# Turning over the expert product of a fused transformer block: activations held, rows of peer_v moving

## The chip, the cores and the metric

The program runs on one core of one Trainium2 chip. The metric is the device time of one launch in microseconds (us). The engines are TensorE (PE, matmuls; PEld is its weight load), VectorE (DVE), ScalarE (ACT), GpSimd (POOL) and the queue of SyncE (SP), which issues most of the loads.

## The reference, cut to what matters

Two transformer blocks in sequence on 512 tokens of width 1024. The part that the change touches is the first block's expert layer (PEER): 16384 experts, each a row of `peer_u` and a row of `peer_v`, both 16384 x 1024, seen as 128 keys of 128 experts. For each token, eight heads pick 16 experts each, with a softmax gate g over the 16. With h the normalised input, the layer adds to the residual

```
x += sum over the chosen experts e of  g[e] * gelu(h . peer_u[e]) * peer_v[e]
```

For one block of 128 tokens the kernel gathers only the chosen rows. For the other 384 tokens it computes the products of all 16384 experts densely, with a gate of zero for those not chosen: first u = gelu(peer_u h), then w = gate x u, then the sum over experts of w times peer_v.

## The kernel before, in words

Everything is kept transposed: x is eight tiles of 128 channels x 512 tokens. Products are float32 made of pairs of fp32r: a value is split into a rounded high part and the rest, and `mm3` (L236) does three matmuls, high x high, high x low and low x high, into one PSUM bank. `wchunk` (L206) loads 128 x 1024 weights (`wraw`, three buffers), copies the high part on ScalarE (`whi`, L214) and takes the difference on VectorE (`wlo`, L215). PSUM has eight banks, handed out by tag: mm 2, S 2, L 2, T 1, st 1 (L89).

`phase_b` (L714) does the expert layer in two stages.

The spill stage: routing on VectorE picks experts and builds the gates of all keys, which are written to DRAM (`Gd`, in 12 writes of 2 MB); meanwhile `u_spill` computes the u products of 68 keys (the first 68, 24 matmuls of 384 columns each) and writes them to DRAM (`Sd`).

The experts stage: `v_group` (L990) handles four keys. It reads their gates (`gt`, 0.75 MB in runs of 512 bytes), reads back the spilled activations (`gr`) or takes those just computed (`gs`), multiplies by the gates (L1002, alternately on VectorE and GpSimd), and splits the result into `whi_` and `wlo_` (L1005, L1006). Then for each of the eight channel chunks m it holds a 128 x 128 piece of peer_v (`pv`, laid out for this on the host) and moves the 384 token columns of the four keys' activations past it: 4 keys x 3 matmuls into one bank S or L, and then one addition to x on VectorE (L1017). 32 groups make 256 such additions. The u products of the other 60 keys (`u_tile`) are woven in between by step counts, and groups of spilled and of fresh keys alternate.

Beside both stages runs `gather` (L914) for the first 128 tokens: an indirect DMA on GpSimd's queue fetches 128 rows (`row`, L927, four buffers), and VectorE multiplies and sums (L938, L945). `weave` advances it by the ratio VR of the costs that the main loop yields, and `pace` ties each of its instructions to a matmul already recorded.

The last group's additions feed the next norm chunk by chunk (`nf.add`: high part and square on ScalarE, difference and sum on VectorE), and the feed-forward stage follows. Instructions are recorded in the order of the generators; at build time a planner orders each engine's instructions by recorded order and by when its own model has their inputs ready. Engines then work in that order.

Of the kernel before, what the change touches and what calls it, by code (L numbers as in the profile page):

```python
# [7 lines left out]
F32 = mybir.dt.float32  # L8
F32R = mybir.dt.float32r
# [4 lines left out]
AF = mybir.ActivationFunctionType  # L14
OP = mybir.AluOpType
# [7 lines left out]
T = 512  # L23
# [15 lines left out]

CAND = [(a, b) for a in range(16) for b in range(16) if (a + 1) * (b + 1) <= 16]  # L40
NC = len(CAND)
GS = 4
NG = 128 // GS
# [12 lines left out]
PT = 12  # L56
SO = 0.5
TB = 8
BC = 2600
GSC = 32768.0  # L60
# [113 lines left out]
class Kern:  # L174
# [539 lines left out]
    def phase_b(self, n2):  # L714
        nc, I, x = self.nc, self.I, self.x
        ACT, V, G = nc.scalar, nc.vector, nc.gpsimd
        ND = T - TG
        NTB = ND // 32
        dp = self.ctx.enter_context(self.tc.tile_pool(name="dram", bufs=1, space=DRAM))
        Gd = dp.tile([NTB, 128, 128, 32], F32, name="gates")  # L720
        Sd = dp.tile([SPILL, 128, ND], F32, name="spill")
        eg = ExitStack()
        gp_ = eg.enter_context(self.pool("gath", "right"))
        er = ExitStack()
# [2 lines left out]
        rp = erq.enter_context(self.pool("route", "right"))  # L727
# [43 lines left out]
        rp = er.enter_context(self.pool("route2", "right"))  # L771
# [4 lines left out]
        spilled = {}  # L776
# [137 lines left out]
        def gather():  # L914

            g2 = gsel0.rearrange("p h s -> p (h s)")
            acc = gp_.tile([128, 1024], F32, name="gacc")
            V.memset(acc, 0.0)
            dots = gp_.tile([128, 128], F32, name="dots")
            junk = gp_.tile([128, 1024], F32, name="junk")  # L920
# [12 lines left out]
            for n, (tab, s) in enumerate(seq):  # L933
                if n + ROWB - 1 < len(seq):
                    issue(n + ROWB - 1)
                row = rows.pop(n)
                if tab == "u":
                    self.pace(V.scalar_tensor_tensor(junk, row, 1.0, hnat, op0=OP.mult, op1=OP.mult,  # L938
                                                     accum_out=dots[:, s:s + 1]), BACK)
                    if s % 16 == 15:  # L940
                        ss = slice(s - 15, s + 1)
                        ACT.activation(dots[:, ss], dots[:, ss], AF.Gelu_apprx_tanh)
                        V.tensor_tensor(dots[:, ss], dots[:, ss], g2[:, ss], op=OP.mult)
                else:
                    self.pace(V.scalar_tensor_tensor(acc, row, dots[:, s:s + 1], acc, op0=OP.mult, op1=OP.add), BACK)  # L945
                yield 1170
            for k in range(2):
                pt = self.ps("T")
                for q in range(4):
                    m = 4 * k + q  # L950
                    nc.tensor.transpose(pt[:, q * 128:(q + 1) * 128], acc[:, m * 128:(m + 1) * 128], self.ident)
                for q in range(4):
                    m = 4 * k + q
                    V.tensor_tensor(x[m][:, :TG], x[m][:, :TG], pt[:, q * 128:(q + 1) * 128], op=OP.add)
                yield 800

        def u_tile(j, pool, spill):
            ps = self.ps("mm")
            yield from self.proj_g(ps, I["u"][j], hhi, hlo, n=ND, cost=490)
            g = pool.tile([128, ND], F32, name="gs", bufs=3 if spill else 2 * GS)  # L960
            ACT.activation(g, ps[:, :ND], AF.Gelu_apprx_tanh)
            if spill:
                ACT.dma_start(Sd[j], g)
            spilled[j] = None if spill else g
            yield 0

        def u_spill():
            for j in range(SPILL):
                yield from u_tile(j, rp, True)

        gat = gather()

# [14 lines left out]
        ev = ExitStack()  # L987
        vp = ev.enter_context(self.pool("vph", "right"))

        def v_group(g, last):  # L990
            gt = vp.tile([128, NTB, GS, 32], F32, name="gt", bufs=2)
            nc.sync.dma_start(gt.rearrange("p a j t -> p a (j t)"),
                              Gd[:, :, g * GS:(g + 1) * GS, :].rearrange("a p j t -> p a (j t)"))
            W = []
            for q in range(GS):
                j = g * GS + q
                s = spilled[j]
                if s is None:
                    s = vp.tile([128, ND], F32, name="gr", bufs=4)
                    nc.sync.dma_start(s, Sd[j])  # L1000
                s3 = s.rearrange("p (a t) -> p a t", t=32)
                (G if q % 2 else V).tensor_tensor(s3, s3, gt[:, :, q, :], op=OP.mult)  # L1002
                a = vp.tile([128, ND], F32R, name="whi_", bufs=2 * GS)
                c = vp.tile([128, ND], F32R, name="wlo_", bufs=2 * GS)
                ACT.activation(a, s, AF.Copy)  # L1005
                V.tensor_tensor(c, s, a.bitcast(F32), op=OP.subtract)  # L1006
                W.append((a, c))
            for mp in range(4):
                whi, wlo = self.wchunk(I["pv"][g, mp].rearrange("p m j d -> p (m j d)"), 1024)
                for m2 in range(2):  # L1010
                    m = 2 * mp + m2
                    ps = self.ps("L" if m2 else "S")
                    for q in range(GS):
                        o = slice((m2 * GS + q) * 128, (m2 * GS + q + 1) * 128)
                        self.mm3(ps[:, :ND], (whi[:, o], wlo[:, o]), W[q], q == 0, q == GS - 1)
                        yield 490
                    V.tensor_tensor(x[m][:, TG:], x[m][:, TG:], ps[:, :ND], op=OP.add)  # L1017
                    if last:
                        nf.add(m, x[m])

        nf = Norm(self, "f1")
        sg = list(range(SPILL // GS))
        ug = list(range(SPILL // GS, NG))
        seq = []
        ns, nu = len(sg), len(ug)
        a = b = 0
        while a < ns or b < nu:
            if a < ns and (b >= nu or (a + SO) * nu <= b * ns):
                seq.append(sg[a])
                a += 1  # L1030
            else:
                seq.append(ug[b])
                b += 1

        def u_all():
            for g in ug:
                for q in range(GS):
                    yield from u_tile(g * GS + q, vp, False)

        def main():  # L1040
            ugen = u_all()
            total = nu * GS * 9
            vsteps = NG * GS * 8
            done, vdone = 0, 0
            for n, g in enumerate(seq):
                need = (ug.index(g) + 1) * GS * 9 if g in ug else 0
                while done < need:
                    yield next(ugen, 0)
                    done += 1
                if n == len(seq) - 1:  # L1050
                    yield None
                for c in v_group(g, n == len(seq) - 1):
                    yield c
                    vdone += 1
                    while done < total and done * vsteps < vdone * total * 1.08:
                        yield next(ugen, 0)
                        done += 1
            for c in ugen:
                yield c

        weave(main(), gat, VR)
        ev.close()
# [487 lines left out]
def layout(i):  # L1550

    f = lambda n: np.asarray(i[n])
# [33 lines left out]
    r["pv"] = c(f("peer_v")[0].reshape(NG, GS, 128, 4, 2, 128).transpose(0, 3, 2, 4, 1, 5))  # L1586
# [73 lines left out]
```

## Time and profile before

| | us |
|---|---|
| median of 3 runs | 2904.09 (2901.44 to 2911.04) |
| the profiled execution | 2895.47 |
| its span, first to last instruction | 2893.7 |
| PE busy | 2810.8 |
| DVE busy | 2011.0 |
| ACT busy | 1158.4 |
| POOL busy | 477.3 |

The profile is one execution. Busy time is the time in which an engine had an instruction; for PE the instructions overlap, and their ends are modelled, so a busy PE can still lose time between starts. Idle time is put down to the event that came last before the waiting instruction. The granted clock of PE (PEclk) is 1.0 at 2.4 GHz and 0.5 at 1.2 GHz, averaged over a stretch. The DMA share is the mean busy share of 16 DMA engines, and can come out a little above 1.

### The profile page before, as it was taken

What the parts mean: (1) busy time and instruction counts of PE and PEld (TensorE: products, weight loads), DVE (VectorE), ACT (ScalarE), POOL (GpSimd) and SP (SyncE); (2) the same over time, 40 slices, a digit from 0 to 9 for tenths busy, and PEclk for the clock granted to TensorE, in tenths of its full rate; (3) what the DMA queues carried; (4) which work ended last, traced back from release to release, by engine and by line L of the source; (5) the groups of instructions that cost most, each with busy time, mean ns of one, the idle gap of its engine ahead of it and who ended that gap; (6) DMA issues with size and microseconds to landing.
All of it is one profiled execution on the core that took longest, in us unless ns stands there. A gap on an engine that the chain in (4) does not pass through costs nothing. (4 is left out here: it accounts for less than half of the span.)

```text
span 2893.7 us, 38745 instructions
## 1 busy us (share of the span) xinstructions
PE 2810.8 (97%) x14599; PEld 2432.8 (84%) x14599; DVE 2011.0 (69%) x3932; ACT 1158.4 (40%) x1719; POOL 477.3 (16%) x350
## 2 busy tenths in 40 slices
PE   8999999999899998999999999999999999999999
PEld 6678777788799998999999999998888866688887
DVE  6752466679999997889898898974443467544432
ACT  5742344333365663333333333342322355533221
POOL 0000000000042234444444444400000000000000
PEclk9999999999899999999999999999999998999999
DMA  4223211332387889999888898833223311122232
GB/s 167 66 75 113 68 52 52 107 104 81 111 313 249 304 310 350 319 305 318 312 304 311 306 311 294 288 120 101 96 93 93 99 66 44 59 95 95 96 103 79
DMA packets 188956, 494.02 MB, mean 171 GB/s; under 512 B 15968, under 2 KB 84704, under 8 KB 187104
## 3 DMA queue, kind: packets, MB, share of 16 engines
q1 hardware_dynamic: 140384, 318.76, 33.2%
q0 software_dynamic: 36864, 134.23, 13.3%
q10 hardware_dynamic: 11520, 38.54, 3.4%
q8 instruction: 115, 1.88, 0.3%
q14 instruction: 73, 0.60, 0.1%
HBM read 450.84 MB, written 40.63 MB: 170 GB/s over the span
## 5 line engine op out<-in xcount | busy, mean ns | idle before, releaser
L214 ACT ACTIVATE whi<-wraw 128x1024 fp32r<-128x1024 f32 x524 | 546.5, 1044 | 1259.4 <-PE mm L239 623.4
L240 PE MATMUL mm<-hhi,wlo 128*128 128x512 f32 (+1 forms) x2272 | 843.9, 372 | 34.9 <-DVE wlo L215 34.8
L238 PE MATMUL mm<-hhi,whi 128*128 128x512 f32 (+1 forms) x2272 | 854.7, 376 | 19.4 <-ACT whi L214 9.0
L239 PE MATMUL mm<-hlo,whi 128*128 128x512 f32 (+1 forms) x2272 | 841.5, 370 | 0.0
L215 DVE TENSOR_TENSOR wlo<-wraw,whi 128x1024 fp32r<-128x1024 f32 x524 | 640.5, 1224 | 241.7 <-ACT whi L214 238.6
L240 PEld LDWEIGHTS mm<-hhi,wlo 128*128 128x128 f32 x2272 | 432.1, 190 | 93.3 <-DVE wlo L215 42.1
L238 PEld LDWEIGHTS mm<-hhi,whi 128*128 128x128 f32 x2272 | 432.5, 190 | 76.6 <-ACT whi L214 10.1
L239 PEld LDWEIGHTS mm<-hlo,whi 128*128 128x128 f32 x2272 | 432.3, 190 | 49.4 <-issue 3.6
L927 POOL DMA_INDIRECT row<-u_nat,eidx x128 | 193.7, 1513 | 584.4 <-PE mm L239 327.9
L927 POOL DMA_INDIRECT row<-v_nat,eidx x128 | 188.3, 1471 | 247.7 <-PE mm L240 56.6
L945 DVE SCALAR_TENSOR_TENSOR gacc<-row,dots,gacc 128x1024 f32<-128x1024 f32 x128 | 171.7, 1342 | 20.8 <-DMA row<-v_nat,eidx 11.1
L938 DVE SCALAR_TENSOR_TENSOR junk<-row,hnat 128x1024 f32<-128x1024 f32 x128 | 164.3, 1284 | 12.6 <-DMA row<-u_nat,eidx 6.6
L238 PE MATMUL mm<-fhi,whi 128*128 128x512 f32 x352 | 139.1, 395 | 0.0
L240 PE MATMUL mm<-fhi,wlo 128*128 128x512 f32 x352 | 139.0, 395 | 0.0
L239 PE MATMUL mm<-flo,whi 128*128 128x512 f32 x352 | 139.0, 395 | 0.0
L884 ACT ACTIVATE stg<-L 128x512 f32<-128x512 f32 x96 | 100.4, 1155 | 46.7 <-PE L L881 37.5
L1083 DVE TENSOR_TENSOR fu<-mm,nbc 128x512 f32<-128x512 f32 x40 | 27.7, 691 | 127.0 <-PE mm L240 127.0
L1079 DVE TENSOR_TENSOR fg<-mm,nbc 128x512 f32<-128x512 f32 x40 | 27.7, 691 | 85.6 <-PE mm L240 84.2
L1017 DVE TENSOR_TENSOR x<-x,L 128x384 f32<-128x384 f32 x128 | 70.2, 548 | 18.5 <-PE L L240 18.1
L240 PEld LDWEIGHTS mm<-fhi,wlo 128*128 128x128 f32 x352 | 66.0, 187 | 16.2
L239 PEld LDWEIGHTS mm<-flo,whi 128*128 128x128 f32 x352 | 66.0, 187 | 16.2
L238 PEld LDWEIGHTS mm<-fhi,whi 128*128 128x128 f32 x352 | 66.0, 187 | 16.1
(2376 smaller groups left out, 4772.5 us busy)
## 6 DMA issues: line engine op xcount, KB each, us to landing
wraw<-u SPq DMA_DIRECT2D x128, 512.0 KB
wraw<-pv SPq DMA_DIRECT2D x128, 512.0 KB
gates<-stg ACTq DMA_DIRECT2D x12, 2048.0 KB
gt<-gates SPq DMA_DIRECT2D x32, 768.0 KB
spill<-gs ACTq DMA_DIRECT2D x68, 192.0 KB
gr<-spill SPq DMA_DIRECT2D x68, 192.0 KB
wraw<-w_f1g SPq DMA_DIRECT2D x22, 512.0 KB
wraw<-w_f1u SPq DMA_DIRECT2D x22, 512.0 KB
```

The source lines that it names most:

```text
L214: nc.scalar.activation(hi[:, :n], raw[:, :n], AF.Copy)
L215: (nc.gpsimd if pool_lo else nc.vector).tensor_tensor(lo[:, :n], raw[:, :n], hi[:, :n].bitcast(F32), op=OP.subtract)
L238: nc.tensor.matmul(ps, a[0], b[0], start=start, stop=False)
L239: nc.tensor.matmul(ps, a[0], b[1], start=False, stop=False)
L240: self.mms.append(nc.tensor.matmul(ps, a[1], b[0], start=False, stop=stop).ins.name)
L884: ACT.activation(stg[:, :, o:o + 4].rearrange("p j t -> p t j"), gp.rearrange("p (t j) -> p t j", t=4), AF.Copy, scale=1.0 / GSC)
L927: self.pace(G.indirect_dma_start(out=rows[n], out_offset=None, in_=I[tab + "_nat"], in_offset=bass.IndirectOffsetOnAxis(ap=eidx[:, s:s + 1 ...
L938: self.pace(V.scalar_tensor_tensor(junk, row, 1.0, hnat, op0=OP.mult, op1=OP.mult, accum_out=dots[:, s:s + 1]), BACK)
L945: self.pace(V.scalar_tensor_tensor(acc, row, dots[:, s:s + 1], acc, op0=OP.mult, op1=OP.add), BACK)
L1017: V.tensor_tensor(x[m][:, TG:], x[m][:, TG:], ps[:, :ND], op=OP.add)
L1079: V.tensor_tensor(g, pg, n.bc, op=OP.mult)
L1083: V.tensor_tensor(u, pu, n.bc, op=OP.mult)
```

## The change

The experts stage is turned over. For each key, a 128 x 128 piece of its activations (128 experts x 128 tokens, three pieces for 384 tokens) is held, and the 512 columns of half a row block of peer_v move past it. The result is tokens x channels, in six banks (three token blocks x two halves; tags S, L, T and S, L, st), summed over all 128 keys in PSUM. At the end the six banks are copied out (alternately ScalarE and VectorE), transposed back in 24 pieces of 128 x 128 on TensorE, and added to x in eight additions. The last three keys do the first half of the channels for all three, then the second.

With it: gates are read for eight keys at a time (1.5 MB, runs of 1024 bytes); all gate products are on VectorE; activations are prepared one key at a time, three keys ahead of their product, and loaded four keys before that; the spilled keys are the first four of each eight and the last four, 68 as before; u products are spread over the keys with a lead of 48 steps. The gather has five row buffers in place of four, writes its product over the row instead of into a tile of its own, and takes bank mm for its transposes; VR goes from 0.345 to 0.335. The copy of peer_v laid out on the host is no longer needed.

```diff
-GS = 4
-SPILL = 68
+GS = 8
+PREP = 3
+LEAD = 48
+TAIL = 3
-ROWB = 4
+ROWB = 5
-VR = 0.345
+VR = 0.335
 ...
+        def slot(j):
+            return j % GS < GS // 2 or j >= T_ALL - GS // 2
 ...
+        def gates_in(g):
+            gts[g] = vp.tile([128, NTB, GS, 32], F32, name="gt", bufs=GTB)
+            nc.sync.dma_start(gts[g].rearrange("p a j t -> p a (j t)"),
                               Gd[:, :, g * GS:(g + 1) * GS, :].rearrange("a p j t -> p a (j t)"))
+        def act_in(j):
+            if slot(j):
+                acts[j] = vp.tile([128, ND], F32, name="gr", bufs=7)
+                nc.sync.dma_start(acts[j], Sd[j])
+        def prep(j):
+            s = acts.pop(j)
+            s3 = s.rearrange("p (a t) -> p a t", t=32)
+            V.tensor_tensor(s3, s3, gts[j // GS][:, :, j % GS, :], op=OP.mult)
+            a = vp.tile([128, ND], F32R, name="whi_", bufs=WB)
+            c = vp.tile([128, ND], F32R, name="wlo_", bufs=WB)
+            ACT.activation(a, s, AF.Copy)
+            V.tensor_tensor(c, s, a.bitcast(F32), op=OP.subtract)
+            W[j] = a, c
+        Y = [[self.ps(t) for t in tags] for tags in (("S", "L", "T"), ("S", "L", "st"))]
+        def v_part(j, h, b):
+            a, c = W[j]
+            whi, wlo = chunks[j]
+            o, bs = slice(h * 512, h * 512 + 512), slice(b * 128, b * 128 + 128)
+            st, sp = j == 0, j == T_ALL - 1
+            y = Y[h][b]
+            nc.tensor.matmul(y, a[:, bs], whi[:, o], start=st, stop=False)
+            nc.tensor.matmul(y, a[:, bs], wlo[:, o], start=False, stop=False)
+            self.mms.append(nc.tensor.matmul(y, c[:, bs], whi[:, o], start=False, stop=sp).ins.name)
 ...
+        def y_add(m):
+            h, q = divmod(m, 4)
+            ps = self.ps("mm")
+            for b in range(3):
+                nc.tensor.transpose(ps[:, b * 128:(b + 1) * 128], yn[h, b][:, q * 128:(q + 1) * 128], self.ident)
+            V.tensor_tensor(x[m][:, TG:], x[m][:, TG:], ps[:, :ND], op=OP.add)
+            nf.add(m, x[m])
 ...
+            n_v = T_ALL - TAIL
+            gates_in(0)
+            loaded = prepped = 0
+            for n in range(n_v + 1):
+                if n < n_v:
+                    if n % GS == GS // 2 and n // GS + 1 < NG:
+                        gates_in(n // GS + 1)
+                    last = T_ALL if n == n_v - 1 else min(n + PREP + 1, T_ALL)
+                    while loaded < min(T_ALL, last + 4):
+                        act_in(loaded)
+                        loaded += 1
+                    while prepped < last:
 ...
+                        prep(j)
+                        prepped += 1
+                if n < n_v:
+                    chunk(n)
+                    for i in range(6):
+                        v_part(n, i // 3, i % 3)
+                        yield 680
+                        yield from u_to(int(len(here) * 8 * min(1.0, (n * 6 + i + LEAD) / (T_ALL * 6))))
+                    del chunks[n]
```

## Rows read from the trace of the kernel before

**Rows 1.** The page: span, and busy time and share of each engine.
```profile
span 2893.7 us, 38745 instructions
...
PE 2810.8 (97%) x14599; PEld 2432.8 (84%) x14599; DVE 2011.0 (69%) x3932; ACT 1158.4 (40%) x1719; POOL 477.3 (16%) x350
```

**Rows 2.** Busy time by stretch: stretch, length, busy (instructions), PEclk, DMA share, GB/s.
```profile
1097.00:1135.00 38.00, 27.99 (x132) 26.83 (x131) 24.71 (x26) 10.64 (x17) 15.63 (x13) 0.82 1.03 377
1135.00:1745.00 610.00, 597.11 (x3396) 590.21 (x3396) 550.22 (x731) 213.37 (x291) 287.85 (x214) 1.00 0.90 310
1745.00:1773.00 28.00, 22.96 (x118) 22.13 (x118) 20.83 (x26) 6.42 (x8) 10.54 (x9) 0.88 0.82 283
1773.00:1912.00 139.00, 138.69 (x800) 138.21 (x799) 118.80 (x164) 49.75 (x67) 48.38 (x35) 1.00 0.74 257
...
1097.00:1927.00 830.00, 801.75 (x4526) 792.33 (x4525) 728.11 (x965) 291.17 (x399) 362.40 (x269) 0.99 0.87 300
```

**Rows 3.** Timeline of PE: start, length, engine, line; each pair starts ten matmuls apart.
```profile
1503.15 0.33 PE L239 MATMUL mm<-hlo,whi 128*128 128x384 f32 x1
...
1504.88 0.33 PE L240 MATMUL mm<-hhi,wlo 128*128 128x384 f32 x1
...
261.67 0.39 PE L240 MATMUL L<-whi,hlo 128*128 128x512 f32 x1
...
263.94 0.39 PE L238 MATMUL S<-whi,hhi 128*128 128x512 f32 x1
...
565.18 0.39 PE L238 MATMUL mm<-ahi,whi 128*128 128x512 f32 x1
...
567.51 0.39 PE L239 MATMUL mm<-alo,whi 128*128 128x512 f32 x1
```

**Rows 4.** Waits of PE, 1135 to 1912 us: total us, times, longest.
```profile
PE mm L240 <- DVE wlo L215: 4.4, 2, 3.1
PE S L240 <- DVE wlo L215: 3.2, 4, 1.9
PE S L238 <- ACT whi__11157 L1005: 1.3, 1, 1.3
...
PE S L238 <- ACT whi__13831 L1005: 0.2, 1, 0.2
```

**Rows 5.** Groups of instructions, 1097 to 1927 us: count, busy, mean ns, idle before.
```profile
L1017 DVE TENSOR_TENSOR x<-x,S 128x384 f32<-128x384 f32 x128 | 70.0, 547 | 7.7 <-PE S L240 7.3
...
L1002 POOL TENSOR_TENSOR gr<-gr,gt 128x384 f32<-128x384 f32 x34 | 43.2, 1272 | 80.7 <-DMA gr<-spill 64.2 <-issue 9.8 <-DVE wlo L215 4.0
...
L1002 DVE TENSOR_TENSOR gs<-gs,gt 128x384 f32<-128x384 f32 x30 | 16.5, 551 | 0.0
```

**Rows 6.** Timeline at the end of the stage and in the next norm.
```profile
1926.57 0.39 PE L238 MATMUL mm<-hhi,whi 128*128 128x512 f32 x1
...
1929.00 0.55 DVE L1017 TENSOR_TENSOR x<-x,L 128x384 f32<-128x384 f32 x1
...
1931.26 0.69 DVE L150 TENSOR_TENSOR acc<-acc,sq 128x512 f32<-128x512 f32 x1
...
1939.53 0.65 PE L169 MATMUL T<-consts,nrn 128*128 128x128 f32 x4
```

**Rows 7.** Timeline at the start of the stage.
```profile
1104.57 0.39 SPq L992 DMA_DIRECT2D gt<-gates  x1
...
1109.02 0.69 PE L240 MATMUL mm<-hhi,wlo 128*128 128x384 f32 x1 [6.90 <-DVE wlo L215]
...
1111.74 0.43 SPq L992 DMA_DIRECT2D gt<-gates  x1
...
1114.78 0.55 DVE L1002 TENSOR_TENSOR gs<-gs,gt 128x384 f32<-128x384 f32 x1
...
1123.45 0.34 PE L238 MATMUL S<-whi__10644,whi 128*128 128x384 f32 x1
```

**Rows 8.** Timeline of VectorE in the disturbed stretch.
```profile
1751.34 0.56 DVE L1002 TENSOR_TENSOR gr<-gr,gt 128x384 f32<-128x384 f32 x1 [2.74 <-DMA gt<-gates]
```

More of the change, by code (lines that the diff above doesn't have):

```diff
@@ L720, in phase_b @@
         Gd = dp.tile([NTB, 128, 128, 32], F32, name="gates")
-        Sd = dp.tile([SPILL, 128, ND], F32, name="spill")
+        Sd = dp.tile([T_ALL, 128, ND], F32, name="spill")
         eg = ExitStack()
@@ L947, in gather @@
             for k in range(2):
[L948 removed]
+                pt = self.ps("mm")
                 for q in range(4):
@@ L959, in u_tile @@
             yield from self.proj_g(ps, I["u"][j], hhi, hlo, n=ND, cost=490)
-            g = pool.tile([128, ND], F32, name="gs", bufs=3 if spill else 2 * GS)
+            g = pool.tile([128, ND], F32, name="gs", bufs=3 if spill else 8)
             ACT.activation(g, ps[:, :ND], AF.Gelu_apprx_tanh)
@@ L965, in u_tile @@
             yield 0
+        def slot(j):
+            return j % GS < GS // 2 or j >= T_ALL - GS // 2
         def u_spill():
-            for j in range(SPILL):
-                yield from u_tile(j, rp, True)
+            for j in range(T_ALL):
+                if slot(j):
+                    yield from u_tile(j, rp, True)
         gat = gather()
@@ L1021, in phase_b @@
-        nf = Norm(self, "f1")
[L1022 to L1030, printed above, removed]
-            else:
[L1032 to L1038, printed above, removed]
+        order = list(range(T_ALL))
@@ new lines, in phase_b @@
+        here = [j for j in order if not slot(j)]
+        gts, acts, W, chunks = {}, {}, {}, {}
+        def gates_in(g):
+            gts[g] = vp.tile([128, NTB, GS, 32], F32, name="gt", bufs=GTB)
+            nc.sync.dma_start(gts[g].rearrange("p a j t -> p a (j t)"),
+                              Gd[:, :, g * GS:(g + 1) * GS, :].rearrange("a p j t -> p a (j t)"))
+        def act_in(j):
+            if slot(j):
+                acts[j] = vp.tile([128, ND], F32, name="gr", bufs=7)
+                nc.sync.dma_start(acts[j], Sd[j])
@@ new lines, in prep, with chunk @@
+        def prep(j):
[7 more added lines that the diff above has]
+            W[j] = a, c
+        def chunk(j):
+            chunks[j] = self.wchunk(I["v_nat"][j * 128:(j + 1) * 128], 1024)
@@ new lines, in phase_b, with y_out @@
+        yn = {}
+        def y_out(h, b):
+            if not yn:
+                yn["t"] = vp.tile([128, NTB, GS, 32], F32, name="gt", bufs=GTB)
+            t = yn["t"].rearrange("p a j t -> p (a j t)")[:, (3 * h + b) * 512:(3 * h + b + 1) * 512]
+            if (h + b) % 2:
+                V.tensor_copy(t, Y[h][b])
+            else:
+                ACT.activation(t, Y[h][b], AF.Copy)
+            yn[h, b] = t
+        def y_add(m):
[5 more added lines that the diff above has]
+            nf.add(m, x[m])
@@ L1040, in main, with u_all @@
         def main():
+            def u_all():
+                for j in here:
+                    yield from u_tile(j, vp, False)
+                    acts[j] = spilled[j]
             ugen = u_all()
[L1042 to L1052, printed above, removed]
-                    yield c
[L1054 to L1057, printed above, removed]
@@ L1058, in main, with u_to @@
-            for c in ugen:
-                yield c
+            done = [0]
+            def u_to(n):
+                while done[0] < n:
+                    c = next(ugen, None)
+                    if c is None:
+                        return
+                    done[0] += 1 if c else 0
+                    yield c
+            n_v = T_ALL - TAIL
[10 more added lines that the diff above has]
+                    while prepped < last:
+                        j = prepped
+                        if not slot(j):
+                            yield from u_to((here.index(j) + 1) * 8)
+                            for c in ugen_end(ugen, j):
+                                yield c
+                        prep(j)
[7 more added lines that the diff above has]
+                    del chunks[n]
@@ new lines, in main @@
+            tail = list(range(n_v, T_ALL))
+            yield None
+            for h in range(2):
+                for j in tail:
+                    if h == 0:
+                        chunk(j)
+                    for b in range(3):
+                        v_part(j, h, b)
+                        yield 680
+                    if h == 1 and j < tail[-1]:
+                        m = j - n_v
+                        y_add(m)
+                for b in range(3):
+                    y_out(h, b)
@@ L1061, in phase_b, with ugen_end @@
+            for m in range(TAIL - 1, 4):
+                y_add(m)
+            for m in range(4, 8):
+                y_add(m)
+        def ugen_end(g, j):
+            while j not in acts:
+                c = next(g, None)
+                yield c or 0
         weave(main(), gat, VR)
```

38 lines of the change are left out of this document (4 added, 34 removed).

## The prediction

> **What bounds the kernel now.** The page comes first: TensorE is busy for 97% of a span of 2893.7 us, VectorE for 69% [rows 1], and the DMA engines, in the longest part of the changed stage, for 0.90 [rows 2]. So whatever this change gives must be TensorE time: either fewer cycles of streaming, or shorter waits of TensorE. A table by stretches then splits the experts stage, 1097 to 1927 us, into its start, two long quiet parts with a disturbed stretch between them, and the end; in each the reader is to compare the number of matmuls with the time [rows 2]. For that I need the time of one matmul in an undisturbed stream, which the durations don't give (they overlap); the starts of successive matmuls do: ten matmuls of 384 columns take 1504.88 - 1503.15 = 1.73 us, so one takes 173.4 ns (the starts are rounded; I use 173.4) [rows 3]. Then 4526 matmuls need 784.8 us of the 830, and 45 us are lost. By stretch (time less number times 173.4 ns): 15 at the start, 21 in the first long part, 7.5 in 1745 to 1773, 0.3 after it [rows 2]. TensorE's own waits between 1135 and 1912 name what is late: eleven waits of 0.2 to 1.3 us (10.6 in sum; the first and the last row are shown) for the copy of a key's activations (whi_ of L1005), and six (7.6 us) for a weight split on VectorE [rows 4].
>
> **The change, part by part.**
>
> *Streaming.* Before, 32 groups x 8 chunks x 4 keys x 3 = 3072 matmuls of 384 columns; after, 128 keys x 2 halves x 3 token blocks x 3 = 2304 of 512. The columns are the same, 1,179,648, so only what a matmul costs beyond its columns can be saved. The trace has the new shape already: in the attention's v projection a weight chunk of 512 columns moves past 128 token columns of activations, and ten matmuls take 263.94 - 261.67 = 2.27 us, 227 ns each; another stream of 512 columns (the branch projection) takes 2.33 us for ten, 233 ns [rows 3]. At the full level of 2.4 GHz, at which this stretch runs, 384 and 512 columns are 160 and 213.3 ns, so about 13.4 ns are left over in both shapes. 3072 x 173.4 = 532.7 us becomes 2304 x 226.7 = 522.3: a gain of 10.4 us. With the slower of the two streams it is 2304 x 233 = 536.8, a loss of 4.1. I take the first, since there a weight chunk is what moves, as here.
> [...]
>
> *Residual adds.* The 256 additions of 384 columns from PSUM (two groups of 128, one of them shown, 0.547 us each) go: 140 us of VectorE [rows 5]. In their place stand six copies out of PSUM, 24 transposes and eight additions at the end. Four transposes in a row took 0.65 us from the first start to the last end [rows 6], so 24 are at most 3.9 us more on TensorE; I take 3, as the last end hangs over.
>
> *Gate products.* The 64 products on GpSimd (1.27 us each in the group shown) go to VectorE at 0.55 us, +35 us there [rows 5]. VectorE, 728 us busy in this stage [rows 2], falls to about 728 - 140 + 35 = 623, from 88% to some 77%. By itself this is worth nothing, since VectorE doesn't set the end. It pays through the queue: the weight splits stand behind less.
>
> *Waits of the long parts.* Activations are now prepared three keys ahead, one key at a time, while four at once were needed at each group's start; three keys are 3 x (18 x 0.227 + 11 x 0.173) = 18 us of TensorE work, and the chain behind one key (a product, a copy and a difference of 384 columns, the product 0.55 us long [rows 5]) is short against that. So I take the 10.6 us of group starts as gone. Of the 7.6 us of waits for splits I keep 3. The rest of the 28.8 us lost there (28.8 - 18.2 = 10.6: half-clock time after the 1754 us wait and matmuls a few ns late) I keep to 7. That leaves 10 in place of 28.8. Bounds: 3 (only the kept waits), and above, all of 28.8 and the bursts of the third rival.
>
> *Gates by eight keys.* 16 reads of 1.5 MB instead of 32 of 0.75. Runs of 1024 bytes in place of 512 may move faster; I count nothing, as the DMA share in the quiet part is 0.90 [rows 2] and it is the waiting, not the sum, that could hurt. SP's queue holds behind each read the loads of spilled activations (seven buffers, so seven keys deep) and the weight chunks (three raw buffers). A product that waits for its gates also holds up the splits behind it on VectorE, and TensorE waits for those.
>
> *Start of the stage.* Before, four u tiles were recorded first and the gates were wanted only afterwards. The gates' read went out at 1104.57, after the last gates write; TensorE stood 6.9 us for a split at 1109.02 (at half clock after it); the first v product came at 1123.45 [rows 7]. After, the first key's preparation stands first, and needs 1.5 MB through a DMA that is full (share 1.03, 377 GB/s [rows 2]). The first 0.75 MB were used at 1114.78, 10 us after the issue [rows 7]; twice as much lands some 2 to 4 us later, and the first product could go at about 1119. The order on an engine is not the recorded one: the second group's read went out at 1111.74, ahead of the first group's products, which are recorded before it [rows 7]. So the u tiles that are recorded next (30 steps of 3 matmuls, 15.6 us) can be put ahead of the first product and fill 1097 to 1113. So about the same 15 us are lost. Bounds: 8 (no wait for the split) and 26 (TensorE does one or two u tiles and then stands until 1119, with half clock after it).
>
> *End.* Before, the residual adds of the last group ran beside its matmuls; the last one came at 1929.00, the last norm sum at 1931.26, and the FFN's first matmuls had begun at 1926.57: TensorE never stood [rows 6]. After, four of eight chunks can only be added when the last matmul is through; each needs an addition (0.55), a split's difference and a norm sum (0.69 [rows 6], and I take as much for the difference), so 1.9 us of VectorE, 8 us in all, with the last copies out of PSUM ahead of them. What hides it is the FFN over the first four chunks: 4 x 3 x 0.227 = 2.7 us for each weight chunk, three chunks at hand. If the planner uses all three it is covered, if none it costs 8 to 9 us: I take 3.
>
> The spill stage before 1097 us writes 68 tiles as before, only others; the in-place product and the fifth row buffer cost nothing there, since the instructions stay the same in number and size, and a row that comes earlier can only shorten a wait.
>
> **Sum.** Streaming 784.8 - 532.7 + 522.3 + 3 = 777.4; waits 15 + 10 + 3 = 28; 805 us in place of 830: 25 us less. The profiled execution took 2895.5 us (span 2893.7 and 1.8 around it), so after it 2870. The median of the runs shown is 2904.1, 8.6 above the profiled one; I predict a median, so 2904 - 25 = 2879 us.
>
> **Rivals.**
> 1. *The streaming saves nothing.* The moving chunk meets the slower cadence of 233 ns (536.8 instead of 522.3, +14.5); what the waits give remains. For it: one of the two streams of 512 columns runs so; against it: the one in which weights move doesn't [rows 3]. 805 + 14.5 = 819.5, 10.5 gained: 2894 us, on the edge of what can be told. Chance 0.16; half of that falls within 0.3%.
> 2. *The waits of the long parts were the DMA's.* With share 0.90 the loads are late whatever VectorE does, and 28.8 us stay in place of 10: 19 less gain, 2898 us, no change. For it: in 1745 to 1773 VectorE itself waited 2.74 us for gates [rows 8]. Against it: TensorE's waits name the preparation of keys much more often [rows 4]. Chance 0.10.
> 3. *Slower: each gates read stops the pipe.* A read of 1.5 MB alone takes about 4 us at 377 GB/s, 8 or more beside row and chunk loads; if the product waits for it, the splits behind it wait, TensorE stands for over 3 us and then runs at half clock. That is what happened once, at 1745 to 1773: a product 2.74 us late for its gates [rows 8], TensorE 3.1 us late for a split [rows 4], granted clock 0.88, 7.5 us lost [rows 2]. A read is recorded only one key (6 us) before its first use. On all 15 later reads it would be 112 us (2991), on six 45 (2924); from four on (30 us) the gain is gone. Against it: SP issues a read as soon as the buffer two groups back is free, some eight keys earlier, as the read at 1111.74 shows [rows 7]. Chance 0.13.
>
> **How the numbers follow.** Forecast 0.61, rivals 0.16, 0.10, 0.13. 2879 is the forecast's time. Its own bounds: all in favour (start 8, middle 3, end 0) is 17 less, 2862; start 26 and end 9 give 17 more, 2896. To hold 8 in 10 the range takes in the first two rivals and the beginning of the third: 2857 to 2908. A measurement of this kernel can tell about 0.3% (8.7 us) from no change: below 2895 is faster, above 2913 slower. Faster: most of the forecast and half of the first rival, 0.68; within: 0.17; slower: 0.15.
>
> **What would show it.** Right: ten v matmuls of 512 columns in 2.27 us; no waits of TensorE for whi_ of the key activations; GpSimd without products; VectorE near 77% in the stage; TensorE's waits in the middle under 10 us; the stage near 805 us. Wrong: 2.33 us for ten; waits of VectorE for gates of several us, followed by half-clock stretches, at every eighth key; a gap of over 15 us ahead of the first v product, or of over 6 after the last.

## The result, and the profile of the changed kernel

The change made the kernel slower: a median of 2940.8 us over four runs (2938.2 to 2953.5) against 2903.9 us for the kernel before beside it, a ratio of 1.0141 (95% interval 1.0118 to 1.0165). 2879 us were predicted, with a range that ended at 2908. The profiled execution took 2941.75 us.

The page of the changed kernel, to be held against [rows 1]. TensorE does 744 matmuls fewer and its busy time is larger; VectorE has 116 us less to do, GpSimd 105 us less.

```profile
span 2940.0 us, 36859 instructions
...
PE 2828.4 (96%) x13855; PEld 2339.4 (80%) x13855; DVE 1894.8 (64%) x3751; ACT 1157.9 (39%) x1722; POOL 372.5 (13%) x286
```

The table by stretches (columns as in [rows 2]): the start of the stage, the part behind it, the whole stage up to the FFN, and 25 us of it cut out.

```profile
1092.00:1130.00 38.00, 25.57 (x113) 23.41 (x112) 22.00 (x26) 9.80 (x16) 10.10 (x9) 0.78 1.01 375
1130.00:1960.00 830.00, 786.23 (x3616) 671.09 (x3615) 576.61 (x736) 269.07 (x368) 239.21 (x196) 0.98 0.82 282
1092.00:1969.00 877.00, 820.24 (x3768) 701.22 (x3766) 604.77 (x770) 285.28 (x392) 249.30 (x204) 0.97 0.83 284
1600.00:1625.00 25.00, 19.49 (x83) 16.56 (x82) 12.76 (x17) 5.38 (x8) 4.89 (x5) 0.86 0.76 268
```

The stage took 877 us where 805 were forecast. VectorE is busy for 605 of them, 69%, less than the 623 that I had worked out, and still TensorE waits for it. The granted clock of the long middle part fell from 1.00 in the quiet part of before [rows 2] to 0.98, and in the 25 us that are cut out it is 0.86. The waits say where that comes from: first those of TensorE, then those of VectorE, 1135 to 1960 us (waiting and released by, total us, times, longest).

```profile
PE mm L243 <- DVE wlo L218: 24.6, 8, 5.5
PE S L1035 <- DVE wlo L218: 18.2, 8, 3.4
PE mm L241 <- ACT whi L217: 0.8, 1, 0.8
```
```profile
DVE gr L1014 <- DMA gt<-gates: 51.9, 13, 6.7
```

The waits for the copies of a key's activations [rows 4] are gone, as predicted. In their place are 16 waits for a weight split, 42.8 us; and VectorE, which makes the splits, stands 13 times, 51.9 us in sum, at a gate product whose gates have not landed. One of the 13, as the timeline of all engines shows it:

```profile
1589.64 0.55 DVE L1014 TENSOR_TENSOR gs<-gs,gt 128x384 f32<-128x384 f32 x1
...
1590.22 0.97 SPq L1002 DMA_DIRECT2D gt<-gates  x1
...
1598.87 1.22 DVE L218 TENSOR_TENSOR wlo<-wraw,whi 128x1024 fp32r<-128x1024 f32 x1
...
1603.13 1.06 ACT L217 ACTIVATE whi<-wraw 128x1024 fp32r<-128x1024 f32 x1 [4.35 <-PE mm L242]
...
1604.84 1.50 DVE L1014 TENSOR_TENSOR gr<-gr,gt 128x384 f32<-128x384 f32 x3 [4.75 <-DMA gt<-gates]
...
1608.32 0.56 DVE L1014 TENSOR_TENSOR gr<-gr,gt 128x384 f32<-128x384 f32 x1 [1.98 <-DMA gr<-spill]
...
1609.94 1.22 DVE L218 TENSOR_TENSOR wlo<-wraw,whi 128x1024 fp32r<-128x1024 f32 x1
...
1611.16 0.55 DVE L1014 TENSOR_TENSOR gs<-gs,gt 128x384 f32<-128x384 f32 x1
...
1611.21 0.69 PE L243 MATMUL mm<-hhi,wlo 128*128 128x384 f32 x1 [5.51 <-DVE wlo L218]
1611.70 0.63 PE L1034 MATMUL T<-whi,whi__14150 128*128 128x512 f32 x1
```

Read it from the last line but one upwards. TensorE stood 5.51 us for a split (wlo) that VectorE began at 1609.94. ScalarE had finished the high part of that weight chunk at 1604.19, so the split could have run then. It stood behind four products of spilled activations (gr), of which the first waited 4.75 us for gates and the last 1.98 us for its activations. The gates' read had gone out at 1590.22, just after the last product of the group two back had freed the buffer (1589.64), and was used 14.6 us later. And those four products were not urgent: they belong to keys 80 to 83, TensorE was at key 71, and the products of the keys between that need no load (gs, 76 to 79) come after them, from 1611.16. After the stall the matmuls last 0.63 to 0.69 us instead of 0.33 to 0.40: the 1.2 GHz level.

Ten matmuls of the turned products in a stretch without u tiles, from TensorE's timeline of the changed kernel; 2.33 us lie between the two starts, where 2.27 were forecast.

```profile
1866.58 0.40 PE L1035 MATMUL st<-wlo,whi__16019 128*128 128x512 f32 x1
...
1868.91 0.40 PE L1036 MATMUL T<-whi,wlo__16090 128*128 128x512 f32 x1
```

The start and the end of the stage in the timeline, beside [rows 7] and [rows 6].

```profile
1100.09 1.28 DVE L947 SCALAR_TENSOR_TENSOR gacc<-row,dots,gacc 128x1024 f32<-128x1024 f32 x1 [5.19 <-DMA row<-v_nat,eidx]
...
1103.03 1.22 DVE L218 TENSOR_TENSOR wlo<-wraw,whi 128x1024 fp32r<-128x1024 f32 x1
1103.23 0.39 SPq L1002 DMA_DIRECT2D gt<-gates  x1
1104.31 0.69 PE L243 MATMUL mm<-hhi,wlo 128*128 128x384 f32 x1 [7.59 <-DVE wlo L218]
...
1115.22 1.55 DVE L1014 TENSOR_TENSOR gr<-gr,gt 128x384 f32<-128x384 f32 x3 [1.86 <-DMA gr<-spill]
...
1116.39 0.50 PE L1034 MATMUL S<-whi,whi__10509 128*128 128x512 f32 x1 [1.92 <-ACT whi__10509 L1017]
...
1967.40 0.39 PE L1036 MATMUL st<-whi,wlo__16896 128*128 128x512 f32 x1
1967.63 0.82 PE L1054 MATMUL mm<-consts,gt 128*128 128x128 f32 x6
1969.19 0.50 PE L241 MATMUL S<-hhi,whi 128*128 128x512 f32 x1 [0.74 <-ACT whi L217]
...
1970.64 1.01 PE L1054 MATMUL mm<-consts,gt 128*128 128x128 f32 x6 [0.72 <-DVE x L1055]
```

The long wait at the start, 7.59 us, has the form of the others. The split at 1103.03 stood behind products of the gather, of which the first had waited 5.19 us for its row; ScalarE was through with the chunk by 1096.04. It was so in the kernel before, too: there a gather product waited 4.84 us for its row (1104.83) ahead of the split for which TensorE stood 6.90 us [rows 7].

**An account of the stage.** To compare kernels I add up the distances between the starts of successive matmuls, from the last u matmul of the spill stage to the 200th matmul of the FFN. *Base* is the matmuls times 173.4 ns (384 columns) and 227 ns (512); *over base* is what undisturbed matmuls (within 12 ns of it) take beyond; *waits* are the idle times that the trace names; *half clock* is the rest of the longer distances. What is lost in the first 45 us or so is the *start*, and stands there alone. Microseconds; the last four kernels are those of experiments 1, 8 and 9 below.

| | before | after | paced | before, VectorE products | the same, padded | change: paced, padded, banks in turn |
|---|---|---|---|---|---|---|
| stage | 876.2 | 928.1 | 877.8 | 858.3 | 858.4 | 869.4 |
| base | 828.0 | 818.3 | 818.3 | 828.0 | 828.0 | 818.3 |
| over base | 3.5 | 15.2 | 15.4 | 4.0 | 0.4 | 10.4 |
| waits, middle | 18.2 | 40.7 | 7.3 | 5.1 | 8.6 | 5.1 |
| half clock, middle | 8.5 | 24.1 | 8.7 | 5.0 | 7.3 | 8.7 |
| start | 15.7 | 21.3 | 17.7 | 14.1 | 12.0 | 17.3 |
| transposes | 1.9 | 6.3 | 6.7 | 1.9 | 1.9 | 6.2 |
| waits and half clock at the end | 0.3 | 2.4 | 3.9 | 0.4 | 0.4 | 3.4 |

The stage grew by 51.9 us: 38.1 in the middle, 5.6 at the start, 4.4 for transposes, 2.1 at the end, and 2.0 in streaming (9.7 less base, 11.7 more over base). The stages before it took 5.0 us less and those after it 0.6 less, which makes the 46.3 us between the spans. The medians lie only 36.9 us apart: the profiled execution of the kernel before was 8.4 us faster than its median, that of the changed kernel 0.9 slower. So the account overstates the loss by some 9 us, and no trace tells in which stage.

### The profile page after: what moved, and what is told of

Read it like the earlier page. It is cut to its first block, busy times and chain, and to the rows that moved or that the text cites. A ratio compares the mean times of both kernels' runs of the same rounds, so it can differ in the third digit from the quotient of the medians.

```text
span 2940.0 us, 36859 instructions
## 1 busy us (share of the span) xinstructions
PE 2828.4 (96%) x13855; PEld 2339.4 (80%) x13855; DVE 1894.8 (64%) x3751; ACT 1157.9 (39%) x1722; POOL 372.5 (13%) x286
## 5 line engine op out<-in xcount | busy, mean ns | idle before, releaser
L243 PE MATMUL mm<-hhi,wlo 128*128 128x512 f32 (+1 forms) x2272 | 848.1, 374 | 51.9 <-DVE wlo L218 51.5
L218 DVE TENSOR_TENSOR wlo<-wraw,whi 128x1024 fp32r<-128x1024 f32 x524 | 628.1, 1200 | 303.2 <-ACT whi L217 299.6
L929 POOL DMA_INDIRECT row<-u_nat,eidx x128 | 182.0, 1422 | 702.1 <-PE mm L242 326.3
L929 POOL DMA_INDIRECT row<-v_nat,eidx x128 | 180.1, 1407 | 372.7 <-DVE gacc L947 77.9
L947 DVE SCALAR_TENSOR_TENSOR gacc<-row,dots,gacc 128x1024 f32<-128x1024 f32 x128 | 163.9, 1280 | 52.3 <-PE mm L243 16.9
L940 DVE SCALAR_TENSOR_TENSOR row<-row,hnat 128x1024 f32<-128x1024 f32 x128 | 156.1, 1220 | 52.9 <-PE mm L243 24.7
L1014 DVE TENSOR_TENSOR gr<-gr,gt 128x384 f32<-128x384 f32 x68 | 35.3, 553 | 70.1 <-DMA gt<-gates 51.9
```

What stands on the lines that cost most here:

```text
L218: (nc.gpsimd if pool_lo else nc.vector).tensor_tensor(lo[:, :n], raw[:, :n], hi[:, :n].bitcast(F32), op=OP.subtract)
L243: self.mms.append(nc.tensor.matmul(ps, a[1], b[0], start=False, stop=stop).ins.name)
L940: self.pace(V.scalar_tensor_tensor(row, row, 1.0, hnat, op0=OP.mult, op1=OP.mult, accum_out=dots[:, s:s + 1]), BACK)
L1014: V.tensor_tensor(s3, s3, gts[j // GS][:, :, j % GS, :], op=OP.mult)
```

## Experiments

Each ran beside the kernel before; ratios are to it, with 95% intervals.

**1. Products placed late.** `pace` makes an instruction wait for the last matmul that is recorded ahead of it, so the planner cannot put it far ahead of its turn.

```
-            V.tensor_tensor(s3, s3, gts[j // GS][:, :, j % GS, :], op=OP.mult)
+            self.pace(V.tensor_tensor(s3, s3, gts[j // GS][:, :, j % GS, :], op=OP.mult))
```

> After, with the gate product of a key tied to the last matmul recorded before it (about four keys ahead of its use), so that it can't stand early in VectorE's queue. Theory A (the planner puts the products of the next group's spilled keys on VectorE some ten keys early, where its model believes the gates landed; they land 14 us after the issue and the weight splits behind the waiting product are late): VectorE's 52 us of waits for gates and TensorE's stall at every eighth key (about 2 to 5.5 us each, then half clock) go; 2875 to 2895 us. Theory B (the 1.5 MB burst itself starves the weight chunks): ScalarE still waits some 40 us for chunks, TensorE still stalls at each read; 2930 to 2945 us.

Measured: 2896.6 us, 0.9976 (0.9960 to 0.9992), 1.6 us above the range of the first theory and far from the second. TensorE's waits and VectorE's longest waits for anything that a product needs, 1135 to 1925 us of the paced kernel:

```profile
PE mm L241 <- ACT whi L217: 4.7, 1, 4.7
PE S L1035 <- DVE wlo L218: 3.3, 2, 1.6
...
DVE gr L1014 <- PE st L1036: 20.2, 21, 1.9
...
DVE gr L1014 <- PE mm L243: 15.2, 12, 2.4
```

VectorE no longer waits for gates at all; its products wait for the matmul that they are tied to, never over 2.4 us. The waits and the half clock of the middle fall from 64.8 to 16.0 us. The matmuls are as slow as before the edit (15.4 us over base). So the place of the products in VectorE's queue is the cause of the loss, and the cadence is a second, separate matter.

**2. The spilled keys' products on GpSimd.** Nothing makes the products later; their waiting is done on an engine that makes no splits.

```
-            V.tensor_tensor(s3, s3, gts[j // GS][:, :, j % GS, :], op=OP.mult)
+            (G if slot(j) else V).tensor_tensor(s3, s3, gts[j // GS][:, :, j % GS, :], op=OP.mult)
```

> After, with the gate products of the 68 spilled keys back on GpSimd (the others stay on VectorE). Theory A: the wait for gates moves to GpSimd's queue, no weight split stands behind it, TensorE's stalls at each read mostly go: 2880 to 2905 us; GpSimd's row fetches wait instead, and VectorE may wait for rows. Theory B: stalls stay, 2930 to 2945 us.

Measured: 2895.5 us, 0.9975 (0.9961 to 0.9990). GpSimd's first wait and TensorE's first two, 1130 to 1925 us:

```profile
POOL gr L1014 <- DMA gr<-spill: 61.4, 8, 15.8
...
PE S L1035 <- DVE wlo L218: 6.1, 4, 3.0
PE mm L243 <- DVE wlo L218: 3.2, 6, 0.9
```

A product may now be up to 15.8 us late and TensorE stands 3.0 us at most. The same waits, off the engine that makes the splits, cost nothing.

**3. No reads after the second.** Groups 2 to 15 use the gates of the two groups that are already there (14 of 16 reads left out, and most keys get another group's gates).

```
-                    if n % GS == GS // 2 and n // GS + 1 < NG:
-                        gates_in(n // GS + 1)
+                    if n == GS // 2:
+                        gates_in(1)
+                    elif n % GS == GS // 2 and n // GS + 1 < NG:
+                        gts[n // GS + 1] = gts[n // GS - 1]
```

> After, with the gates of the first two groups used for all later groups too: 14 of 16 gates reads are left out (and the gates of those keys are wrong). Both theories: no stall at every eighth key; the DMA share falls by some 0.08. It bounds what the reads cost in all: about 2870 to 2890 us. If it stays above 2920, the stalls are not the gates'.

Measured: 2902.4 us, 0.9999 (0.9987 to 1.0011), 38 us better than the change, but not the 2870 to 2890 expected. What VectorE's products wait for then, 1130 to 1925 us:

```profile
DVE gr L1014 <- DMA gr<-spill: 35.1, 22, 3.5
```

With 14 of the 16 reads left out it is no faster than with all of them and paced products. VectorE still waits 35.1 us, for spilled activations, but never over 3.5 us, and the middle loses only 19.4 us. The reads' traffic is not what costs.

**4. Reads half as large.** Gates by four keys, four buffers of 0.75 MB, with the reads issued every four keys.

```
+GQ = 4
 ...
-            gts[g] = vp.tile([128, NTB, GS, 32], F32, name="gt", bufs=GTB)
+            gts[g] = vp.tile([128, NTB, GQ, 32], F32, name="gt", bufs=2 * GTB)
 ...
-                    if n % GS == GS // 2 and n // GS + 1 < NG:
-                        gates_in(n // GS + 1)
+                    if n % GQ == 0 and n // GQ + 1 < T_ALL // GQ:
+                        gates_in(n // GQ + 1)
```

> After, with the gates read by four keys (0.75 MB, four buffers in place of two, recorded one key ahead as before); products unpaced, all on VectorE. If the size of the read makes the waits: a read lands in half the time, VectorE's 52 us of waits for gates fall below 20 and TensorE's middle waits from 41 to under 20 us; about 2905 us. If it is only that products stand early on VectorE, whatever the size: more but shorter waits, the sum near 50 us and the time near 2935.

Measured: 2943.7 us, 1.0135 (1.0112 to 1.0158), as slow as the change. VectorE's wait for the products, and TensorE's, 1130 to 1975 us:

```profile
DVE gr L1015 <- DMA gr<-spill: 69.6, 29, 6.3
...
PE mm L244 <- DVE wlo L219: 23.5, 8, 5.1
PE S L1036 <- DVE wlo L219: 19.0, 9, 3.5
```

The waits for gates fall from 51.9 us to 9.2 (three of them), and the early products wait for the spilled activations instead, as long as before. So it isn't the size of the read: whichever load comes last holds the queue.

**5. 32 bytes at the foot of the right-hand pools.** In the built programs every undisturbed stream of 512 columns that comes at 233 ns has one of its two tiles, the moving or the held one, at an address that leaves 32 on division by 64; the streams at 227 ns have both at multiples of 64. In most of the slow streams it is the moving tile. In the turned products it is the held one, a key's activations: the weight chunk that moves lies at a multiple of 64 already. A tile of 32 bytes ahead of the right-hand pools shifts these activations and most of the other slow tiles.

```
+        self.padp = ctx.enter_context(self.pool("pad", "right"))
+        nc.vector.memset(self.padp.tile([128, 8], F32, name="pad"), 0.0)
```

> After, with one unused tile of 32 bytes per partition at the base of the right-hand memory, which moves the stage's activation tiles (and the FFN's) from addresses that are 32 modulo 64 bytes to multiples of 64; instructions the same. If the address makes the cadence of 233 ns: the 2304 v matmuls and the FFN's second product (1056 matmuls) come at 227 ns, 13 + 6 us less, about 2920 us. If the roles or the change of banks make it: 233 ns and 2941 us.

Measured on the changed kernel: 2935.1 us, 1.0109 (1.0074 to 1.0144), 6 less than without the pad where 20 were expected, and the two intervals overlap. The same pad with a second one for the left-hand pools, on the kernel before:

> The kernel before, with two unused tiles of 32 bytes per partition (one at the base of the right-hand memory, one in the left), so that all large tiles start at multiples of 64 bytes. If a moving tile of 512 columns at 32 modulo 64 costs 6.6 ns per matmul: the streams of the FFN's second product, the branch and output projections and the query projection (about 2100 matmuls) come at 227 ns, about 13 us less, 2889 us; the v products of 384 columns stay at 174 ns. If addresses don't matter: 2903.

Measured: 2886.0 us, 0.9938 (0.9921 to 0.9956). Ten matmuls of an FFN stream in the kernel before (first fence) and in that with both pads (second), from TensorE's timeline: 2.33 and 2.26 us. Over the whole profiled execution the matmuls of 512 columns lie 15.2 us over 227 ns each without the pads and 1.8 with them.

```profile
2518.83 0.40 PE L240 MATMUL mm<-yhi,wlo 128*128 128x512 f32 x1
...
2521.16 0.40 PE L238 MATMUL mm<-yhi,whi 128*128 128x512 f32 x1
```
```profile
2518.25 0.39 PE L238 MATMUL mm<-yhi,whi 128*128 128x512 f32 x1
...
2520.51 0.39 PE L239 MATMUL mm<-ylo,whi 128*128 128x512 f32 x1
```

In the changed kernel the pad brings the turned products to 226.7 ns too, in the stretches where they run alone (median over all stretches of ten there). Between u tiles of 384 columns they stay at 230 to 233, whichever the address, so the stage gets back 5 us of the 12.6 that they lie over base. In the profiled execution the stage fell by 7.6 us and what follows it by 8.1, while the part before it was 5.7 longer; that the median gained only 6 is left at that.

**6. Paced and padded.**

> After, with the paced gate products of e1 and both pads. If the two causes add: 2897 less 5 (v cadence, as e2 showed it) less some 13 (the other streams), 2876 to 2884 us. If the waits found other places: 2890 or more.

Measured: 2880.5 us, 0.9920 (0.9902 to 0.9938). The two repairs add up.

**7. Another bank at every matmul.** The remaining cadence might have been three matmuls in a row into one PSUM bank.

```
+        for r in range(3):
+            term, k = divmod(3 * i + r, 6)
+            h, b = divmod(k, 3)
...
+            nc.tensor.matmul(Y[h][b], l[:, bs], m[:, o], start=j == 0 and term == 0, stop=False)
```

> e6, with a key's 18 v matmuls in another order: all six banks with the first product, then all six with the second, then the third, so that the bank changes at every matmul and not at every third. If the change of bank makes what is left of the cadence (230.3 in place of 227 ns with aligned tiles, some 10 ns per change): 236 to 238 ns, 14 to 18 us more than e6. If not: the cadence stays at 230 ns and the time is e6's.

Measured: 2870.3 us, 0.9894 (0.9876 to 0.9912), but not for that reason: the distance over the whole middle stays at 230.3 ns (7.7 us over base against 7.5). It waits 3 us less in the middle, and 4.3 of its gain lie in a stage far behind this one, the second block's attention, where nothing was edited. There both kernels stand 3.87 us for the same copy; behind it, experiment 6 does 22 matmuls more at the 1.2 GHz level (successive starts of 512 columns 0.43 us apart where this kernel has 0.23, and a granted clock of 0.64 against 0.83 over 25 us). That is a shorter stretch at half clock and not less streaming. Of the 13 profiled executions only this one and the second of this kernel (experiment 9) have it; why the clock rises earlier in them is open.

**8. The kernel before, with the GpSimd products on VectorE.** One part of the change alone.

```
-                (G if q % 2 else V).tensor_tensor(s3, s3, gt[:, :, q, :], op=OP.mult)
+                V.tensor_tensor(s3, s3, gt[:, :, q, :], op=OP.mult)
```

> The kernel before, with the 64 gate products that GpSimd did moved to VectorE (the same products, nothing else changed). Theory A, in its wide form (any product on VectorE that can come early for its gates or its spilled activations holds up the weight splits behind it): GpSimd's 64 us of waits for spilled activations appear on VectorE, TensorE's waits between 1135 and 1912 us go from 18 to 35 or more with half clock behind them, 2925 us or more. Theory A, narrow form (only the change's order, with products recorded one key at a time and a group's spilled keys first, lets them come early; before, the four keys of a group are prepared together and VectorE already does two of them without waiting): VectorE waits under 10 us for loads, TensorE's waits stay at 18 +- 6, the time within 0.3% of the kernel before, 2895 to 2913 us.

Measured: 2882.3 us, 0.9938 (0.9914 to 0.9962), faster than either theory had it. TensorE's waits, 1135 to 1912 us, and what VectorE's products wait for:

```profile
PE S L240 <- DVE wlo L215: 4.4, 2, 2.5
PE S L238 <- ACT whi__10659 L1005: 2.5, 1, 2.5
...
DVE gr L1002 <- DMA gr<-spill: 5.8, 4, 2.6
...
DVE gr L1002 <- DMA gt<-gates: 3.2, 1, 3.2
```

The eleven waits for a key's copy [rows 4] are gone, with nothing else changed; one of 2.5 us, at the first group, is new. All eleven had been for the fourth key of a group, whose product was on GpSimd. The timeline of before around the first of them (its wait of TensorE is the 1.3 us in [rows 4]):

```profile
1182.30 1.23 DVE L215 TENSOR_TENSOR wlo<-wraw,whi 128x1024 fp32r<-128x1024 f32 x1 [0.40 <-ACT whi L214]
1182.72 1.66 POOL L1002 TENSOR_TENSOR gs<-gs,gt 128x384 f32<-128x384 f32 x1 [1.63 <-ACT gs L961]
1183.44 2.02 DVE L938 SCALAR_TENSOR_TENSOR junk<-row,hnat 128x1024 f32<-128x1024 f32 x1
...
1184.41 0.52 ACT L1005 ACTIVATE whi__11157<-gs 128x384 fp32r<-128x384 f32 x1 [1.77 <-POOL gs L1002]
```

The chain from the gelu over the product to the copy is what was late, and on VectorE the product takes 0.55 us [rows 5] where it took 1.66. And although all 128 products now stand on VectorE, GpSimd's 64.2 us of waits for spilled activations [rows 5] come to 9.0 us there (5.8 for activations, 3.2 for gates): in the order of before the products are not far ahead of their loads. Which part of the new order brings them forward (the mixture of spilled and other keys in a group, or one key at a time) was not tried.

**9. Both kernels at their best, side by side.** The kernel before with experiments 5 and 8 together, and experiment 7 once more.

> The kernel before, with the 64 gate products moved from GpSimd to VectorE and with both 32-byte pads: two edits that gained 0.62% each when made alone, and no v product turned over. If the two gains are independent (one takes TensorE's waits at the starts of groups away, the other shortens the matmuls of 512 columns in other stages), the time is 2903.9 x 0.9938 x 0.9938 = 2868 us (2861 to 2876). Rival: both draw on the same time (a stream that runs faster meets later splits), then 2880 us or more.

> The best version of the change so far (products paced, both pads, a bank changed at every matmul) once more, beside the kernel before with both edits. Theory: turning the v products over is worth nothing by itself (2304 x 230.3 ns + 4 us of transposes = 535 us against 3072 x 173.4 ns = 533 us), so the two kernels lie within 0.3% of each other, both near 2870 us. Rival: the turned order has a gain of its own (no additions to the residual between the matmuls, activations prepared one key at a time): it is faster by 9 us or more.

Measured: 2872.5 us, 0.9898 (0.9883 to 0.9913), and 2872.3 us, 0.9906 (0.9891 to 0.9922). Both beat the two kernels of this case, and by their medians they are level: turning the products over brings nothing that the medians can tell. The gains of experiments 5 and 8 come to 1.02% together, where 1.24% would be their sum; the time lies in the range given for independent gains, and a small overlap of the two is not excluded. By the account the turned stage is 11 us longer (10.0 over base, 5.3 at the start, 4.3 for transposes, 3.0 at the end, against 9.7 less base and 2.1 less loss in the middle); spans of 2868.5 and 2870.1 us come out level, since in its profiled execution the part before the stage took 5.2 less and the part behind it 4.2 less. Neither is shown to come from the turning: in the 13 profiled executions the stage begins anywhere between 1090.6 and 1102.9 us, and the 4.2 are the shorter stretch at half clock of experiment 7. The turned stage by itself is the slower one in this pair.

## Why the prediction was wrong

*The step that failed* is that of the gates by eight keys, together with the waits of the long parts: the sum has 10 us there and nothing for the gates, and 64.8 were lost (40.7 of waits, 24.1 at half clock). Of the 72 us by which the stage exceeded its forecast (877 against 805) this term is some 55, the streaming 12, the start 6. I saw the danger (a product that waits for its gates holds up the splits behind it), priced it at up to 112 us and gave it 0.13. My reason against it was that the read goes out eight keys ahead. That was so, but it compared the read with the *need*. What counts is the product's place in VectorE's queue, and the planner put the spilled keys' products of the next group nine keys ahead of their need, right behind the read. The row that I used for the read [rows 7] says that order on an engine isn't the recorded one; I took it for the one instruction where it helped and not for the product. The third rival happened at 13 of 15 reads, at a smaller price than the 7.5 us that I had: 38.1 us more waits and half clock in the middle, 2.9 each. Experiments 1 to 4 show it from four sides: late products, products elsewhere, and no reads each take it away, smaller reads don't.

The mechanism is the queue. The Trainium skill (PSUM — Partial Sum Buffer, "Engine vs sequencer instructions") says that the queues of ScalarE, VectorE and GpSimd are strict FIFO; the trace agrees, as the split whose chunk was ready at 1604.19 goes at 1609.94, after the last waiting product.

*Gate products.* "By itself this is worth nothing" was wrong, and I gave its gain to another part. In the order of before it is worth 17.9 us of the stage (experiment 8). I had read the eleven waits for copies as four keys prepared at once; their names would have told that each is a fourth key, and the rows of GpSimd's products how long the step before the copy takes [rows 5].

The Trainium skill (SBUF — State Buffer, "Summary: rules for kernel authors") has a rule that bears on this: a GpSimd operation that reads SBUF beside a VectorE operation with two SBUF inputs is blocked until that one ends, and the other way round. The trace of before agrees, both ways. In the lines of experiment 8 GpSimd's product, begun beside a split that ended at 1183.53, took 1.66 us, and the gather's operation begun beside that product took 2.02, where those that overlap no product took 1.22. Of the stage's 189 splits on VectorE the 42 that overlap a product on GpSimd took 1.52 us in the mean, the other 147 took 1.22 and none over 1.23; with the products off GpSimd (experiment 8) the mean of all is 1.22. So the prediction's 623 us for VectorE did not reckon with some 28 us by which GpSimd's products had lengthened VectorE's splits and gather operations in the stage; 605 were measured. How much of the 17.9 us is owed to this blocking, and how much to the longer product, was not separated.

*Streaming.* The slower cadence of the first rival came: 2.0 us lost instead of 10.4 won. I chose between two rows by what was moving, weights or activations. In the row that I took, both tiles lie at multiples of 64; here the held activations don't, and I hadn't looked at addresses. That decides for a part (experiment 5), and for another part the mixture with matmuls of 384 columns, which no row of mine had.

*Residual adds and VectorE's load* fell, the load further than worked out, and helped nothing: an engine at 69% held TensorE up more than at 88%. *Transposes* cost 4.4 where I took 3. *The start* lost 5.6 more; it stayed within its bounds of 8 and 26, but there was a wait of 7.59 us for a split, as before, and another of 1.92 for the first key's copy, ahead of the first product. That long wait came from the gather's rows, which no step of mine had. *The end* cost 2.1, where 3 were taken. The other steps of this paragraph were right in mechanism.

## What to carry to other kernels

Before work is moved to an engine that feeds the bottleneck, ask for each moved instruction what it waits for and what stands behind it in that engine's queue; a low busy share says nothing about it. When a planner orders the queue, tie an instruction that can wait for a load to the moment at which it is needed, or put it on an engine that feeds nothing urgent. And make the parts of a large change one by one: here one line was worth 0.6%, the alignment of the pools 0.6%, and the large rewrite around them nothing that the medians can tell.

## What was not expected of the hardware

A matmul of 512 columns whose moving and held tiles both begin at multiples of 64 bytes is taken up every 226.7 ns; with one of the two 32 bytes beside such an address it takes 233.3, and either one is enough. In the changed kernel, some 1900 such matmuls in undisturbed streams have the moving tile beside, some 500 the held one. No stream of 512 columns here has both beside, so it is open whether each address counts or the 32 bytes between the two. Two unused tiles of 32 bytes moved whole stages from one cadence to the other (0.62% of the kernel before, experiment 5). With 384 columns the difference is about a nanosecond (3.1 us over the 3072 matmuls of the stage whose moving tile the pads shift). And matmuls of 512 columns that alternate with ones of 384 take 230 to 233 ns at either address; its cause is open.

VectorE's splits take 1.52 us in the mean beside a product on GpSimd and 1.22 without one (kernel before), so a helper engine can slow the engine that it relieves.
